# Sixteen loads of a state space layer kept in program order on GpSimd's DMA queue

## The chip, the cores and the metric

The kernel runs on one core of a Trainium2 chip. The core has five engines that work side by side, each through its own list of instructions in the order of that list: TensorE (PE in the profile; its weight loads are PEld), VectorE (DVE), ScalarE (ACT), GpSimd (POOL) and SyncE (SP, which here only issues DMAs). Sixteen DMA engines move data between the device memory and the on-chip memory; they serve DMAs issued from SP (queue q1 in the profile), from POOL (q0) and from ACT (q10). The metric is the device time of one execution in microseconds (us).

## The reference, cut to what matters

Four layers and then a fifth, more complex one act on 256 tokens of 1024 features. Each layer is a mixer and a gated feed-forward network (FFN) with a short convolution. The mixers of the first four layers are attention, spatial gating, a state space layer and attention. The state space layer is the one that the change touches:

```
def s5_layer(xn, w_in, lam_re, lam_im, log_dt, b_re, b_im, c_re, c_im, d_skip, w_glu):
    u = (xn @ w_in)                       # 64 groups of 16 inputs, 64 complex states each
    bu = einsum(bbar, u)                  # bbar from lam, dt, b
    x  = associative_scan(a, bu)          # along the 256 tokens
    y  = einsum(c, x).real + d_skip * u
    a, g = split(gelu(y) @ w_glu)
    return a * sigmoid(g)
```

## The kernel before, in words

**Stages.** `PHASES` lists eleven stages that run one after the other: sb0, ffn0, sgu, ffn1, s5, ffn2, sb3, ffn3, mix2, ffnx, ple. In all of them TensorE multiplies the activations, split in a high and a low part (`yh`, `yl`), with weights split in the same way (`wh`, `wl`), three products for each 128x128 block (`mm3`, lines 516 to 518).

**The weight stream.** All weights lie in device memory in the order of their use, in units of eight blocks, 512 KB each. SP loads one unit after the other into one of five staging tiles `st` (line 352). ScalarE rounds it to `wh` (line 374), VectorE subtracts to get `wl` (line 375), and the unit's 24 matmuls follow. A staging tile is free for the next load once its unit is split; units are split up to three ahead of the one in use.

**The preparation of the state space layer.** Much of that layer depends on its parameters alone. The generators `s5_pre`, `s5_pre2`, `s5_tables` and `s5_direct` are chained to one list of steps, and `pre_step` (line 419) traces a few of them at a time, at lower priority, between the work of the stages ahead of s5. They put three things in device memory: the output operators `dC`, the input operators `dB` (`s5_pre2`, line 1107) and the terms `dK`, the direct response of outputs to recent inputs.

**The input operators.** `s5_pre2` goes over eight pieces. For each it loads two tiles `A` of 512 KB over GpSimd's queue (lines 1116 and 1118; the next piece's loads are traced a piece ahead), combines them on VectorE in six operations (lines 1128 to 1136), and stores two tiles `O` of 256 KB to `dB`, again over GpSimd's queue (line 1138). The pools hold four `A` and three `O` tiles.

**The direct terms.** `s5_direct` (line 1196) comes last in the chain. It reads `dK` back in 16 loads of 256 KB, eight for each of the two tiles `dT`, over GpSimd's queue (line 1204). One load fills 16 partitions, each with 32 runs of 128 consecutive float32 values, that is runs of 512 bytes. The tiles are used by `y_mm(h, True)` at line 1302, the steps T0 and T1 of stage s5.

**What sets the order.** The program is traced once; the framework's scheduler then orders each engine's list by its own plan of when an instruction's inputs are there, and by priority. The order in which instructions were traced isn't kept, unless an edge says so. `issue_after(ins)` and `keep_in_program_order(ins)` add such edges. `keep_in_program_order` puts its instruction behind the last one that was traced on the same engine: an edge of issue order alone, without a wait for that instruction to end. In `pre_step`, steps of the preparation are put behind the last traced instruction of VectorE and of ScalarE, but not of GpSimd, so that GpSimd's DMAs of a later step can stand ahead of those of an earlier step.

Of the kernel before, what the change touches and what calls it, by code (L numbers as in the profile page):

```python
# [283 lines left out]
class Build:  # L284
# [911 lines left out]
    def s5_direct(s):  # L1196

        while s.cpT is None:
            yield None
        for h in range(2):  # L1200
            s.dT[h] = s.cpT.tile([128, 32, 128], F32, tag="dT%d" % h, name="dT")
            src = s.dK[h * 32:h * 32 + 32, 0:16].rearrange("g h z k -> h g (z k)")
            for j in range(8):
                s.nc.gpsimd.dma_start(s.dT[h][j::8], src[:, :, (8 - j) * 16:(8 - j) * 16 + 128])
                yield DTC

    def s5(s, nxt):
# [740 lines left out]
```

## Time and profile before

| | |
|---|---|
| median of 3 runs | 1618.14 us (1615.52 to 1618.92) |
| the profiled execution | 1621.75 us, of which 1619.9 us is the span from its first to its last instruction |
| TensorE busy | 1574.6 us, 97% of the span |
| VectorE busy | 1303.2 us, 80% |
| ScalarE busy | 948.5 us, 59% |
| GpSimd busy | 68.9 us, 4% |
| mean granted TensorE clock | 0.991 of full speed |
| moved by DMA | 312.55 MB, of which 27.12 MB on GpSimd's queue |

The shares are means over stages with different limits. Stage ffn1, in which the change acts, runs from about 395 to 585 us of the span; s5 follows. In a row of the trace the columns are start, duration, engine, line, operation, what it writes and reads, and in square brackets the time for which the engine stood idle just before it, with what ended that. Matmuls are pipelined: at full clock one ends every 0.11 us, though each is shown with about 0.28 us.

### The profile page before, as it was taken

To read this page: it belongs to the slowest core of one execution; us is meant where nothing else is said; L and a number is where in the kernel's file an instruction comes from. 1 tells how busy PE (TensorE), PEld (TensorE's weight loads), DVE (VectorE), ACT (ScalarE), POOL (GpSimd) and SP (SyncE) were. 2 spreads that over 40 slices of the span, in tenths; PEclk is the share of its full clock that TensorE was granted. 3 is DMA by queue.
4 is the path that set the end of the run, shared out by engine and by line. 5 is a ranking of instruction groups with operands and counts; after the bars stand their busy time and mean duration, and the time that the engine had idled before them with its cause. 6 is when DMAs were issued, how large, how long until landed. Compare 5 with 4: busy or idle time off the path is not lost.

```text
span 1619.9 us, 33923 instructions
## 1 busy us (share of the span) xinstructions
PE 1574.6 (97%) x13644; PEld 1512.5 (93%) x13644; DVE 1303.2 (80%) x2380; ACT 948.5 (59%) x1481; POOL 68.9 (4%) x118
## 2 busy tenths in 40 slices
PE   7999999989999997999999999999999999999998
PEld 6999999979999996999999999999997899999998
DVE  8999998888999877788788558988886667766666
ACT  6777665645556651666566676655665546554444
POOL 0320100021120000000000000000000000000000
PEclk9999999999999997999999999999999999999999
DMA  7655767697996666756665434666554434666662
GB/s 262 202 172 178 232 210 224 198 298 222 263 252 229 219 194 201 259 173 207 196 195 187 153 129 144 203 201 195 159 174 137 149 112 133 200 192 193 195 195 79
DMA packets 95359, 312.55 MB, mean 193 GB/s; under 512 B 15057, under 2 KB 20689, under 8 KB 95201
## 3 DMA queue, kind: packets, MB, share of 16 engines
q1 hardware_dynamic: 82560, 282.21, 55.1%
q0 software_dynamic: 8480, 27.12, 5.9%
q8 instruction: 107, 1.75, 0.4%
q10 hardware_dynamic: 4160, 1.05, 0.3%
q14 instruction: 52, 0.42, 0.1%
HBM read 297.49 MB, written 12.85 MB: 192 GB/s over the span
## 4 chain that ended last, share of the span: by engine, by line
PE 72%; DVE 10%; issue 9%; DMA 5%; ACT 3%; POOL 0%; DVEq 0%; POOLq 0%; ACTq 0%; SPq 0%
PE mm L516 16%; PE mm L518 15%; PE mm L517 15%; PE z L517 5%; PE z L516 5%; PE z L518 5%; DVE wl L375 3%; DMA A<-s5bT_dram 1%; DMA st<-ffn_dram 1%; PE mm L530 1%; PE mm L531 1%; PE mm L529 1%; ACT wh L374 1%; PE z L818 1%; PE z L805 1%
## 5 line engine op out<-in xcount | busy, mean ns | idle before, releaser
L375 DVE TENSOR_TENSOR wl<-st,wh 128x1024 fp32r<-128x1024 f32 x508 | 618.2, 1220 | 156.1 <-ACT wh L374 155.3
L374 ACT CAST wh<-st 128x1024 fp32r<-128x1024 f32 x508 | 528.7, 1046 | 328.0 <-PE mm L517 207.3
L516 PE MATMUL mm<-yh,wh 128*128 128x256 f32 x2512 | 703.7, 280 | 2.9 <-ACT yh L568 1.9
L517 PE MATMUL mm<-yl,wh 128*128 128x256 f32 x2512 | 698.6, 278 | 1.4 <-DVE yl L569 0.9
L518 PE MATMUL mm<-yh,wl 128*128 128x256 f32 x2512 | 698.4, 278 | 1.0 <-DVE wl L375 1.0
L516 PEld LDWEIGHTS mm<-yh,wh 128*128 128x128 f32 x2512 | 473.5, 189 | 10.7 <-issue 6.4
L517 PEld LDWEIGHTS mm<-yl,wh 128*128 128x128 f32 x2512 | 474.1, 189 | 3.3 <-DVE yl L569 1.7
L518 PEld LDWEIGHTS mm<-yh,wl 128*128 128x128 f32 x2512 | 474.1, 189 | 1.7 <-DVE wl L375 1.6
L516 PE MATMUL z<-hh,wh 128*128 128x256 f32 x880 | 243.6, 277 | 0.3 <-ACT hh L542 0.3
L517 PE MATMUL z<-hl,wh 128*128 128x256 f32 x880 | 243.0, 276 | 0.4 <-DVE hl L543 0.4
L518 PE MATMUL z<-hh,wl 128*128 128x256 f32 x880 | 242.1, 276 | 0.0
L516 PEld LDWEIGHTS z<-hh,wh 128*128 128x128 f32 x880 | 165.1, 188 | 1.4 <-ACT hh L542 0.5
L517 PEld LDWEIGHTS z<-hl,wh 128*128 128x128 f32 x880 | 165.2, 188 | 0.6 <-DVE hl L543 0.6
L518 PEld LDWEIGHTS z<-hh,wl 128*128 128x128 f32 x880 | 164.8, 188 | 0.0
L727 DVE SCALAR_TENSOR_TENSOR cv<-pr,conv,cv 128x255 f32<-128x255 f32 (+1 forms) x352 | 147.1, 480 | 0.4
L542 ACT CAST hh<-hm 128x256 fp32r<-128x256 f32 x110 | 44.4, 405 | 121.5 <-DVE hm L732 96.6
L725 ACT ACTIVATE cv<-pr,conv 128x256 f32<-128x256 f32 x176 | 95.7, 593 | 16.6 <-DVE pr L722 16.6
L516 PE MATMUL mm<-oh,wh 128*128 128x256 f32 x320 | 89.8, 282 | 0.0
L517 PE MATMUL mm<-ol,wh 128*128 128x256 f32 x320 | 88.2, 277 | 0.0
L518 PE MATMUL mm<-oh,wl 128*128 128x256 f32 x320 | 88.2, 277 | 0.0
L722 DVE TENSOR_TENSOR pr<-mm,rrow 128x512 f32<-128x512 f32 x88 | 60.3, 689 | 13.1 <-PE mm L518 12.9
L543 DVE TENSOR_TENSOR hl<-hm,hh 128x256 fp32r<-128x256 f32 x110 | 46.0, 422 | 22.7 <-ACT hh L542 22.5
(453 smaller groups left out, 1848.2 us busy)
## 6 DMA issues: line engine op xcount, KB each, us to landing
st<-ffn_dram SPq DMA_DIRECT2D x264, 512.0 KB, 4.3
st<-ffnx_dram SPq DMA_DIRECT2D x66, 512.0 KB, 3.6
st<-sbqk_dram SPq DMA_DIRECT2D x32, 512.0 KB, 4.0
st<-sbv_dram SPq DMA_DIRECT2D x16, 512.0 KB, 4.3
st<-sbo_dram SPq DMA_DIRECT2D x16, 512.0 KB, 3.5
st<-s5glu_dram SPq DMA_DIRECT2D x16, 512.0 KB, 6.1
st<-m_g_dram SPq DMA_DIRECT2D x16, 512.0 KB, 3.6
st<-ple_dram SPq DMA_DIRECT2D x10, 512.0 KB, 3.6
```

The source lines that it names most:

```text
L374: a = s.nc.scalar.copy(t[1][:, :n], t[0][:, :n])
L375: b = s.nc.vector.tensor_tensor(t[2][:, :n], t[0][:, :n], t[1][:, :n].bitcast(F32), OP.subtract)
L516: s.pinned(mm(P, w[0], xh, start=st, stop=False, skip_group_check=True))
L517: mm(P, w[0], xl, start=False, stop=False, skip_group_check=True)
L518: mm(P, w[1], xh, start=False, stop=sp, skip_group_check=True)
L529: s.pinned(mm(P[t][:, :width], a, w[0], start=c == 0, stop=False))
L530: mm(P[t][:, :width], a, w[1], start=False, stop=False)
L542: s.nc.scalar.copy(h, src)
L543: s.nc.vector.tensor_tensor(l, src, h.bitcast(F32), OP.subtract)
L722: nc.vector.tensor_tensor(pr, P, s.rrow.unsqueeze(1).to_broadcast([128, 2, T]), OP.mult)
L725: nc.scalar.activation(hc[:, m], pr[:, m], AF.Identity, bias=w(m, 3), scale=w(m, 2))
L727: nc.vector.scalar_tensor_tensor(hc[:, m, k:], pr[:, m, :T - k], w(m, 2 - k), hc[:, m, k:], OP.mult, OP.add)
```

## The change

Each of the sixteen `dT` loads gets an edge of issue order behind what was traced before it on GpSimd: the first behind the last store of `dB`, each other one behind the load before it.

```
--- before.py
+++ after.py
@@ -1201,7 +1201,8 @@
             s.dT[h] = s.cpT.tile([128, 32, 128], F32, tag="dT%d" % h, name="dT")
             src = s.dK[h * 32:h * 32 + 32, 0:16].rearrange("g h z k -> h g (z k)")
             for j in range(8):
-                s.nc.gpsimd.dma_start(s.dT[h][j::8], src[:, :, (8 - j) * 16:(8 - j) * 16 + 128])
+                s.tc.keep_in_program_order(
+                    s.nc.gpsimd.dma_start(s.dT[h][j::8], src[:, :, (8 - j) * 16:(8 - j) * 16 + 128]))
                 yield DTC
```

## Rows read from the trace of the kernel before

**Rows 1.** The page: busy time of the engines, and shares of the last chain
```profile
PE 1574.6 (97%) x13644; PEld 1512.5 (93%) x13644; DVE 1303.2 (80%) x2380; ACT 948.5 (59%) x1481; POOL 68.9 (4%) x118
PE 72%; DVE 10%; issue 9%; DMA 5%; ACT 3%; POOL 0%; DVEq 0%; POOLq 0%; ACTq 0%; SPq 0%
```
**Rows 2.** GpSimd's instructions in order of time, 390 to 600 us
```profile
390.84 0.56 POOL L1118 DMA_DIRECT2D A<-s5bT_dram  x1
396.92 1.26 POOL L1204 DMA_DIRECT2D dT<-dK  x2 [5.52 <-issue]
...
448.06 1.28 POOL L1204 DMA_DIRECT2D dT<-dK  x2
464.43 1.12 POOL L1138 DMA_DIRECT2D dB<-O  x2 [15.09 <-DVE O L1136]
465.55 1.28 POOL L1204 DMA_DIRECT2D dT<-dK  x2
467.39 3.71 POOL L1204 DMA_DIRECT2D dT<-dK  x6 [0.56 <-issue]
590.27 0.26 POOL L1225 MEMSET S<- 128x16 f32 x4 [119.17 <-PE z L518]
```
**Rows 3.** Tile dT: its uses and its loads (count: ns min/median/max, first and last start)
```profile
L1302 PE MATMUL z<-dT,U x128: 272/273/297, 617.7 to 635.2; 128*32 128x128 f32 x128
L1204 POOL DMA_DIRECT2D dT<-dK x16: 625/643/672, 396.9 to 470.5; - x16
```
**Rows 4.** VectorE's wait for loaded A tiles: sum, times and longest; the longest itself
```profile
DVE O L1128 <- DMA A<-s5bT_dram: 7.5, 3, 5.2
...
395.26 0.69 DVE L1128 TENSOR_TENSOR O<-A 128x512 f32<-128x512 f32 x1 [5.18 <-DMA A<-s5bT_dram]
```
**Rows 5.** Stretches: length, busy (count) by engine, PEclk, DMA share, GB/s
```profile
395.00:465.00 70.00, 65.97 (x544) 64.12 (x543) 68.19 (x127) 42.62 (x66) 11.13 (x20) 0.98 0.91 258
...
470.00:485.00 15.00, 15.00 (x135) 15.00 (x134) 12.24 (x26) 5.18 (x8) 1.10 (x2) 1.00 1.03 239
485.00:500.00 15.00, 13.59 (x114) 13.00 (x113) 14.52 (x25) 9.23 (x13) 0.00 (x0) 1.00 0.87 285
...
540.00:560.00 20.00, 20.00 (x179) 20.00 (x178) 17.40 (x28) 12.00 (x18) 0.00 (x0) 1.00 0.73 231
```
**Rows 6.** DMA queues from 470 to 485 us: packets, MB, share of 16 engines
```profile
q0 software_dynamic: 527, 1.72, 53.6%
q1 hardware_dynamic: 499, 1.85, 48.9%
```
**Rows 7.** ScalarE's rounding of weight units, order of time
```profile
471.73 1.05 ACT L374 CAST wh<-st 128x1024 fp32r<-128x1024 f32 x1
476.85 1.05 ACT L374 CAST wh<-st 128x1024 fp32r<-128x1024 f32 x1 [4.08 <-DMA st<-ffn_dram]
480.83 1.06 ACT L374 CAST wh<-st 128x1024 fp32r<-128x1024 f32 x1 [1.93 <-DMA st<-ffn_dram]
...
485.39 1.06 ACT L374 CAST wh<-st 128x1024 fp32r<-128x1024 f32 x1 [2.30 <-DMA st<-ffn_dram]
488.71 1.05 ACT L374 CAST wh<-st 128x1024 fp32r<-128x1024 f32 x1 [1.27 <-DMA st<-ffn_dram]
```
**Rows 8.** TensorE's waits behind that, order of time
```profile
487.76 0.39 PE L518 MATMUL mm<-yh,wl 128*128 128x256 f32 x1 [0.19 <-DVE wl L375]
491.62 0.39 PE L518 MATMUL mm<-yh,wl 128*128 128x256 f32 x1 [0.82 <-DVE wl L375]
```
**Rows 9.** Shorter stretches, columns as in rows 5
```profile
460.00:465.00 5.00, 5.00 (x47) 5.00 (x46) 5.00 (x9) 3.15 (x5) 0.57 (x2) 1.00 0.53 172
...
398.00:400.00 2.00, 0.92 (x6) 0.69 (x6) 2.00 (x6) 1.63 (x4) 0.19 (x1) 1.00 1.03 252
400.00:402.00 2.00, 1.06 (x4) 0.86 (x5) 2.00 (x5) 2.00 (x5) 0.00 (x0) 0.86 0.92 182
402.00:404.00 2.00, 2.00 (x12) 2.00 (x11) 2.00 (x5) 0.84 (x1) 0.00 (x0) 0.50 0.95 186
...
488.00:490.00 2.00, 2.00 (x19) 2.00 (x19) 2.00 (x6) 1.14 (x2) 0.00 (x0) 1.00 1.02 404
```

## The prediction

> **What bounds the kernel now.** I began with the page's busy times and its last chain: TensorE is busy for 97% of the span and carries 72% of the chain [rows 1]. So a change gains only what it takes from TensorE's few pauses, and costs what it adds to them. An average over the span doesn't say where the pauses are; so next I read GpSimd's list in order of time, to see where the moved loads stand. Of the sixteen `dT` loads the first two are issued at 396.92 us, right behind an `A` load of the input operators, and the last eight at 465.55 us and later, behind the last store of `dB` at 464.43 us [rows 2]. So eight of the sixteen are already where the change wants them, and the other eight go out between 397 and 450 us, ahead of or among the input operators' DMAs. All are there long before TensorE first reads them at 617.7 us [rows 3]. Then I read stretches around both halves. From 540 to 560 us, with no such load, TensorE does 179 matmuls in 20 us, 0.112 us each; a weight unit of 24 then takes 2.68 us, and the stream must bring 0.524 MB in that time, 196 GB/s [rows 5]. From 470 to 485 us, with the last eight `dT` loads under way, the sixteen DMA engines are full (share 1.03) and move only 239 GB/s [rows 5]: 1.85 MB for the stream, 123 GB/s, and 1.72 MB for GpSimd's queue, 115 GB/s [rows 6]. There the stream falls behind its consumer. ScalarE's roundings of the units are to be read as a clock of what arrives: from 471.73 to 485.39 us come three more units, 4.55 us apart, and each of the last four roundings shown waited for its own DMA [rows 7]. TensorE then waits for `wl` at 487.76 and 491.62 us [rows 8], and in the 15 us from 485 us it does 114 matmuls where 134 would fit: 2.2 us lost [rows 5].
>
> **The change part by part.** It removes no work. It moves eight loads, 2.10 MB, from the stretch 397 to 450 us to the end of the row that leaves from 465.55 us on, and adds no wait for an end. The issue itself is short: 0.643 us a load on GpSimd, 10.3 us for sixteen [rows 3]. Behind them on GpSimd stands nothing until a memset at 590.27 us [rows 2], so nobody queues behind the pinned loads; and moved past `dB` stores and `A` loads they free GpSimd for 5 us that it had to spare, as it idles 15.09 us ahead of the last stores alone [rows 2].
>
> What it **gives** is what the eight loads cost where they stood. The thing to ask is whether VectorE ever waited for an `A` tile that stood behind a `dT` load. It waited for `A` three times, 7.5 us in all; the longest wait, 5.18 us, ended at 395.26 us, before the first `dT` load was issued at 396.92 us [rows 2, 4]. It is the costly one, as the residual of the layer's end stands behind it on VectorE, but a load that isn't there yet can't have made it. I find no such wait behind a `dT` load, and so take 0 for this part. Its bounds: in the 70 us from 395 us TensorE does 544 matmuls where 627 would fit, so 9.2 us are lost there, to the end of one layer and the normalisation of the next [rows 5]. That is the most that a better order of VectorE's list could give back, as the scheduler makes its plan anew with the `A` tiles earlier in it; the same shuffle could cost something, and I put 2 us to that side, an estimate from the 2.2 us of the other disturbed stretch [rows 5].
>
> What it **costs** is a longer train of loads at the end: sixteen in a row where there were eight. Eight take 2.10 MB at 115 GB/s = 18.3 us, and in that time the stream runs at 123 of the 196 GB/s that it needs [rows 5, 6]. So each microsecond of the train puts the stream 1 - 123/196 = 0.37 us behind: 6.8 us for eight loads, 13.6 us for sixteen. The units in the staging tiles and those split ahead cover a part. How much, the train of before tells: 6.8 us of lag, 2.2 us of it lost on TensorE, so the cover was 4.6 us. With sixteen, 13.6 - 4.6 = 9.0 us are lost, 6.8 us more than before. The price from the roundings is close: at 4.55 us a unit [rows 7] the lag is 0.41 us per microsecond, 7.5 us for the eight that are added. From below: five staging tiles and three units split ahead are 8 x 2.68 = 21 us of weights, more than the whole lag. If all that were full and usable, nothing would be lost, and the 2.2 us of before would go too: -2.2 us. I take 6.8 us, because the train of before also began after a calm stretch (DMA share 0.53 from 460 to 465 us [rows 9]), when the stream had no more free tiles to fill, and still used its cover up.
>
> A starved TensorE may **lose its clock** too. Where it was busy for 0.92 and 1.06 of 2 us, at 398 to 402 us, the next 2 us were granted at 0.50, the lower of the two levels, 1.2 instead of 2.4 GHz, with 12 matmuls instead of 18: 0.7 us [rows 9]. In the train TensorE would work 2.68 of 4.3 us, 63%; from 485 to 500 us it did 85% of its work at 1.00 [rows 5]. This lies between the two; I take nothing for it, and up to 3 us (four such episodes) for the upper end.
>
> The lag lasts: behind the train TensorE is the bound again (20.00 of 20 us busy [rows 5]), so what it lost there ends the kernel later. The profiled execution took 1621.75 us, of it 1619.9 us span, 3.6 us above the median of 1618.14 us. On it the sum is 1621.75 + 6.8 = 1628.6 us; on the median, 1618.1 + 6.8 = 1624.9 us.
>
> A rule to weigh here is the cost of short runs. By rows, the stream alone moves 404 GB/s at 488 to 490 us [rows 9], and with the 512-byte runs of `dT` beside it both together get 239 GB/s [rows 5]. The Trainium skill, "DMA: Bandwidth & Descriptors", section Specifications, gives 512 bytes as the shortest transfer that still runs at line rate. By that rule the `dT` loads would be no slower than the stream's, and the lag would vanish; the rows above speak against it.
>
> **The rivals.** *The train is covered or harmless*: the time stays. One way is more cover: with eight loads fewer ahead of it the stream could enter the train with more units split. For it: 21 us of room. Against it: the calm stretch right before the old train. It would give between 1618.1 - 2.2 = 1615.9 and 1618.1 + 3.2 us; chance 0.12. Another way is that `dT` loads aren't the slow kind: at 404/2 = 202 GB/s for each queue [rows 9] the stream would have its 196 GB/s and lose nothing, 1615.9 us; against it stands the 239 GB/s at full DMA engines [rows 5]. This is where the rule on 512-byte runs would lead. Chance 0.05. The third is that the edges do little, because the plan for the first eight changes only on paper, and the train spreads: 1618 us, chance 0.05, as the edges are plain and half the loads must move.
>
> *Faster*: VectorE's backlog is what really makes TensorE late in both places, and the new plan removes it. VectorE is busy for 68.19 of 70 us from 395 us [rows 5], and the second wait of TensorE, at 491.62 us, was for a `wl` whose unit was rounded by 489.76 us, 488.71 + 1.05 [rows 7, 8]. If the operators' steps run earlier, the layer boundary gets back up to 9.2 us and the splits keep up in the train, which then costs between 0 and 6.8 us: 1609 to 1616 us, 1612 us in the middle. It decides from the point where an `A` tile that stood behind a `dT` load is on VectorE's path; I see none. Chance 0.10.
>
> **How the numbers follow.** Forecast 1624.9 us, chance 0.68; its own range is 1621.4 to 1630. Covered or harmless 0.12 + 0.05 + 0.05 = 0.22; faster 0.10. The range for 8 in 10 goes from 1616 us (the covered cases) to 1630 us (6.8 + 0.7 from the other pace + 3 for the clock, and 1.4 of the 2 us for a worse order); it leaves out most of the faster case and a little above. About 0.2%, 3.2 us, is what a measurement can tell from no change: faster by more 0.10, within it 0.22, slower by more 0.68.
>
> **What would show it.** All sixteen `dT` issues in one row on GpSimd behind the last `dB` store, some 10 us long, from about 465 us; DMA share at 1.0 with some 240 GB/s for about 37 us instead of 18 us; roundings of units some 4.3 to 4.5 us apart for nine units rather than four; TensorE some 9 us short of its matmuls between 485 and 515 us, against 2.2 us; the stretch 395 to 465 us unchanged at some 544 matmuls; the span's end later by what this stretch lost. It would be wrong if TensorE stays full through the train (more cover than I take), if the clock falls in it (more loss), or if the stretch 395 to 465 us holds clearly more matmuls (a better order of VectorE).

## The result, and the profile after

The changed kernel is slower, as forecast. Its median is 1623.95 us (8 runs, 1620.31 to 1628.46) beside 1615.8 us for the kernel before (8 runs, 1614.91 to 1618.92): the ratio is 1.0051, 95% interval 1.0039 to 1.0062, so +8.15 us, between +6.3 and +10.0. The profiled execution, the slowest of the eight, is counted for the kernel after and not for the one before; without it the difference is 7.5 us. Held against each other instruction by instruction, the two programs differ in GpSimd's list alone; TensorE, ScalarE, VectorE and SyncE have the same instructions in the same order.

| | before | after |
|---|---|---|
| median | 1615.8 us | 1623.95 us |
| profiled execution | 1621.75 us | 1628.46 us |
| its span | 1619.9 us | 1626.7 us |
| end of VectorE's longest wait for `A` to GpSimd's memset of `S` | 195.01 us | 203.54 us |

The last row is the stretch in which the `dT` loads run: it starts where the longest wait of [rows 4] ends, and ends with the memset at the end of [rows 2], which waits for the last product of the feed-forward layer. The first of its ends in the profile after is this row, VectorE in order of time:

```profile
395.81 0.69 DVE L1128 TENSOR_TENSOR O<-A 128x512 f32<-128x512 f32 x1 [5.22 <-DMA A<-s5bT_dram]
```

GpSimd's list in order of time, profile after (start, duration, line, operation; in brackets the idle time ahead of it and what ended it):

```profile
446.40 1.15 POOL L1138 DMA_DIRECT2D dB<-O  x2 [10.38 <-DVE O L1136]
462.52 0.54 POOL L1138 DMA_DIRECT2D dB<-O  x1 [14.98 <-DVE O L1135]
463.15 0.65 POOL L1205 DMA_DIRECT2D dT<-dK  x1
463.79 0.55 POOL L1138 DMA_DIRECT2D dB<-O  x1
464.33 3.75 POOL L1205 DMA_DIRECT2D dT<-dK  x6
468.56 0.64 POOL L1205 DMA_DIRECT2D dT<-dK  x1 [0.48 <-DMA dT<-dK]
470.44 0.62 POOL L1205 DMA_DIRECT2D dT<-dK  x1 [1.25 <-DMA dB<-O]
473.42 0.62 POOL L1205 DMA_DIRECT2D dT<-dK  x1 [2.35 <-DMA dT<-dK]
...
487.44 0.62 POOL L1205 DMA_DIRECT2D dT<-dK  x1 [1.73 <-DMA dT<-dK]
...
599.35 0.26 POOL L1226 MEMSET S<- 128x16 f32 x4 [111.28 <-PE z L518]
```

No `dT` load is left between 397 and 450 us [rows 2]. The first stands ahead of the last `dB` store, the other fifteen behind it: its edge is to the store that was traced last, which the scheduler issued first of the two, at 462.52 us. Seven go out at once; from the eighth on each is held back, seven of these nine by the landing of an earlier `dT` load, so that the issues last until 488 us. Nothing is queued behind them until the memset, which comes 9.1 us later than in [rows 2].

Stretches of the profile after, columns as in [rows 5], and below them the one of before that [rows 5] doesn't have:

```profile
395.00:465.00 70.00, 65.92 (x545) 64.10 (x545) 68.98 (x129) 42.83 (x67) 7.87 (x15) 0.98 0.76 238
...
470.00:485.00 15.00, 15.00 (x135) 15.00 (x133) 9.26 (x22) 5.07 (x8) 3.75 (x6) 1.00 1.03 228
485.00:500.00 15.00, 10.11 (x75) 8.82 (x74) 10.51 (x18) 5.18 (x8) 1.25 (x2) 1.00 1.04 237
500.00:520.00 20.00, 18.39 (x136) 18.10 (x137) 17.60 (x29) 14.30 (x20) 0.00 (x0) 0.83 0.79 238
...
540.00:560.00 20.00, 20.00 (x179) 20.00 (x178) 17.67 (x28) 13.22 (x21) 0.00 (x0) 1.00 0.66 212
```

```profile
500.00:520.00 20.00, 20.00 (x177) 19.83 (x176) 18.90 (x32) 15.72 (x22) 0.00 (x0) 1.00 0.62 202
```

From 395 to 465 us the count of matmuls is the same, 545 and 544; from 540 us on TensorE is full in both. Between 485 and 520 us, where 134 + 179 = 313 matmuls would fit, after does 75 + 136 = 211 and before 114 + 177 = 291: 102 and 22 short, at 0.112 us each 11.4 and 2.5 us, a difference of 9.0 us. That is where the time went. The DMA engines are full all the while (1.03, 1.04) and move 228 and 237 GB/s. By queue, 470 to 485 us (packets, MB, share of the 16 engines), profile after:

```profile
q0 software_dynamic: 510, 1.67, 54.5%
q1 hardware_dynamic: 470, 1.72, 48.4%
```

The stream gets 1.72 MB in 15 us, 115 of the 196 GB/s that it needs. ScalarE's roundings of weight units show the same, profile after, in order of time:

```profile
472.90 1.05 ACT L374 CAST wh<-st 128x1024 fp32r<-128x1024 f32 x1 [2.06 <-DMA st<-ffn_dram]
477.32 1.05 ACT L374 CAST wh<-st 128x1024 fp32r<-128x1024 f32 x1 [3.37 <-DMA st<-ffn_dram]
482.95 1.05 ACT L374 CAST wh<-st 128x1024 fp32r<-128x1024 f32 x1 [3.58 <-DMA st<-ffn_dram]
...
503.82 1.04 ACT L374 CAST wh<-st 128x1024 fp32r<-128x1024 f32 x1 [2.98 <-DMA st<-ffn_dram]
```

These are four of eight roundings, each after a wait for its own DMA: 7 intervals in 30.92 us, or 4.42 us a unit, where TensorE takes 2.68 us for one. TensorE's waits follow from 486.30 us on; two of the six in the profile after (the second is for `hh`, which ScalarE rounds only behind the late unit that it starts at 499.49 us):

```profile
486.30 0.39 PE L518 MATMUL mm<-yh,wl 128*128 128x256 f32 x1 [1.09 <-DVE wl L375]
...
500.90 0.58 PE L516 MATMUL z<-hh,wh 128*128 128x256 f32 x1 [2.89 <-ACT hh L542]
```

Behind the longest hole the clock falls, which before didn't happen here. Short stretches of the profile after:

```profile
500.00:502.50 2.50, 0.89 (x2) 0.60 (x3) 1.93 (x4) 0.84 (x2) 0.00 (x0) 0.60 1.03 231
502.50:505.00 2.50, 2.50 (x13) 2.50 (x13) 1.27 (x3) 1.18 (x2) 0.00 (x0) 0.50 1.01 270
505.00:507.50 2.50, 2.50 (x14) 2.50 (x14) 2.50 (x5) 2.01 (x4) 0.00 (x0) 0.54 1.04 408
```

From 502.5 to 507.5 us TensorE is never idle, but at a granted clock of 0.50 and 0.54, the lower level of 1.2 GHz, it does 27 matmuls where 5/0.112 = 44.6 would fit: 2.0 us of the 11.4, if the weights were there for more, which these rows don't show.

### The profile page after: what moved, and what is told of

Same layout as the page of the kernel before. It is cut to its first block, busy times and chain, and to the rows that moved or that the text cites. A ratio compares the mean times of both kernels' runs of the same rounds, so it can differ in the third digit from the quotient of the medians.

```text
span 1626.7 us, 33926 instructions
## 1 busy us (share of the span) xinstructions
PE 1577.5 (97%) x13644; PEld 1513.8 (93%) x13644; DVE 1303.7 (80%) x2380; ACT 948.8 (58%) x1481; POOL 68.8 (4%) x118
## 4 chain that ended last, share of the span: by engine, by line
PE 69%; DVE 10%; issue 10%; DMA 7%; ACT 3%; POOL 0%; SPq 0%; DVEq 0%; ACTq 0%; POOLq 0%
PE mm L516 15%; PE mm L518 15%; PE mm L517 15%; PE z L517 5%; PE z L516 5%; PE z L518 5%; DVE wl L375 4%; DMA st<-ffn_dram 2%; DMA A<-s5bT_dram 1%; PE mm L530 1%; ACT wh L374 1%; PE mm L531 1%; PE mm L529 1%; DMA st<-m_qk_dram 1%; DMA U<-dU 1%
```

## The experiments

**Theory:** the stream of weights starves in proportion to the train of `dT` loads behind the last store; beyond a cover that eight loads use up, each load costs some 0.85 us and more where the clock falls. **Rivals:** the order of the operators' transfers on GpSimd's queue has a price or gain of its own; the 512-byte runs of a load are what makes it slow; or the DMA engines are simply at their limit at some 240 GB/s.

Each edit is shown against the changed kernel. Beside medians (4 to 12 runs each) the runs are compared in the stretch of the table above, since profiled executions differ ahead of it by up to 4.5 us (its start lies between 391.29 and 395.81 us) although nothing is changed there. A stretch comes from a single profiled execution.

| kernel | stretch | against before | median against before, measured beside it | other engines' lists |
|---|---|---|---|---|
| after | 203.54 us | +8.5 | +8.15 | as before |
| twelve in the train | 198.64 us | +3.6 | +4.4 | as before |
| 32 loads | 213.15 us | +18.1 | +27.1 | changed |
| 16 KB runs | 204.89 us | +9.9 | +10.4 | as before |
| issued by ScalarE | 195.38 us | +0.4 | +8.5 | changed |
| 16 adjacent partitions | 214.83 us | +19.8 | +19.9 | as before |
| 128 partitions, 512-byte runs | 192.16 us | -2.9 | -5.0 | as before |
| 128 partitions, 64 loads of 64 KB | 192.17 us | -2.8 | -5.3 | as before |
| the same, without edges | 194.41 us | -0.6 | +0.5 | as before |
| loads spread in time | 192.32 us | -2.7 | +3.0 | changed |

Where only GpSimd's list differs, the median follows the stretch within 2.5 us. Where the scheduler made another list for TensorE, ScalarE or VectorE, the median is 6 to 9 us above it, lost behind the stretch (1032.4 to 1034.9 us from the memset to the end of the span, against 1023.4 to 1029.6 us with unchanged lists); such runs are read by the stretch alone. With 32 loads and with loads spread in time these lists part from those of before only at 585 us or later, behind the train or behind the stretch. With ScalarE as issuer they part at 491.9 us, and 14 matmuls fewer stand ahead of the memset, so that its stretch comes out some 1.6 us too short.

**Twelve loads behind the last store**, four left free.

```diff
-                dma(dB[pc, :, r], z.rearrange("p g q -> p (g q)"))
+                s.last_db = dma(dB[pc, :, r], z.rearrange("p g q -> p (g q)"))
...
-                s.tc.keep_in_program_order(
-                    s.nc.gpsimd.dma_start(s.dT[h][j::8], src[:, :, (8 - j) * 16:(8 - j) * 16 + 128]))
+                with s.tc.issue_after(s.last_db.ins) if h or j > 3 else nullcontext():
+                    s.nc.gpsimd.dma_start(s.dT[h][j::8], src[:, :, (8 - j) * 16:(8 - j) * 16 + 128])
```

> Only 12 of the 16 direct-term loads are put behind the last store of the input operators; the first four leave early, as before the change. Train theory (every load in the train puts the weight stream behind by 2.29 us x 0.37 = 0.85 us, some 1.0 us with the clock): 4 loads more in the train than before, 3 to 5 us over the kernel before, half of the change's 8.15 us. Rival threshold (the loss comes only once the train is as long as with 16): within 1 us of before. Rival place (the loss comes from the order among the input operators' transfers, which here is half kept): no reason for a half, 0 or 8 us.

Measured: 1619.79 us beside 1615.39 us, ratio 1.0031 (1.0018 to 1.0043). Stretches:

```profile
470.00:485.00 15.00, 14.17 (x125) 13.98 (x124) 10.56 (x20) 6.29 (x10) 1.88 (x3) 1.00 1.04 241
485.00:500.00 15.00, 11.95 (x90) 10.59 (x89) 12.31 (x22) 7.18 (x10) 0.00 (x0) 1.00 0.95 280
```

TensorE is 10 and 44 matmuls short of 135 and 134, and 2 more up to 520 us: 56, or 6.3 us, against 2.5 us with eight in the train and 11.4 us with sixteen. Half the added loads, about half the added time: the price is that of the number behind the store, not of the edge.

**Every load twice**, 32 in the train.

```diff
+        for h in (0, 1, 0, 1):
             src = s.dK[h * 32:h * 32 + 32, 0:16].rearrange("g h z k -> h g (z k)")
...
-                yield DTC
+                yield DTC / 2
```

> Every direct-term load is made twice, 32 in one train behind the last store. Train theory: 16 more loads x 2.29 us x 0.37 = 13.6 us more than the change's 8.15 us, and more pauses in which the clock may fall: 21 to 27 us over the kernel before. Rival once (the loss is a one-time price for emptying the staging tiles or for GpSimd's waits): 8 to 10 us over before, as with 16.

Measured: 1642.5 us beside 1615.39 us, 1.0171 (1.0154 to 1.0189). Stretches:

```profile
485.00:500.00 15.00, 9.61 (x58) 8.31 (x57) 8.80 (x15) 5.38 (x8) 4.51 (x7) 0.84 1.04 240
500.00:520.00 20.00, 18.16 (x140) 17.36 (x140) 13.09 (x22) 10.61 (x15) 5.14 (x9) 0.93 1.04 237
520.00:540.00 20.00, 16.87 (x123) 15.47 (x122) 11.90 (x19) 8.51 (x14) 0.49 (x1) 0.94 1.03 257
```

The full DMA engines and the starved TensorE last to 540 us. Stretch by stretch the sixteen loads more cost 18.1 - 8.5 = 9.6 us, 0.6 us each, somewhat under the 0.85 us of the prediction; the rest of the 27.1 us comes behind the stretch, where the lists are others, and no row ties it to the train.

**Long runs.** Sixteen runs of 16 KB a load instead of 512 bytes; `dT` gets other values.

```diff
-            src = s.dK[h * 32:h * 32 + 32, 0:16].rearrange("g h z k -> h g (z k)")
...
-                s.tc.keep_in_program_order(
-                    s.nc.gpsimd.dma_start(s.dT[h][j::8], src[:, :, (8 - j) * 16:(8 - j) * 16 + 128]))
+                g0 = h * 32 + (j % 4) * 8
+                src = s.dK[g0:g0 + 8].rearrange("g (a b) z k -> (g a) (b z k)", a=2).rearrange("p (g k) -> p g k", k=128)
+                s.tc.keep_in_program_order(s.nc.gpsimd.dma_start(s.dT[h][j::8], src))
```

> The 16 loads stay where the change puts them and carry the same 256 KB each, but read it as 16 runs of 16 KB in place of 512 runs of 512 bytes, from other addresses of the same tensor; so the values of the direct terms are others. Theory short runs (the train costs because 512-byte runs fill the DMA engines at 239 GB/s): the stream gets some 200 GB/s beside the loads and keeps up; the train takes some 21 us, and the time is 0 to 2 us under the kernel before. Rival shared queue (any second queue takes half of a fixed total of 240 GB/s): 8 us over before, as with short runs.

Measured: 1625.77 us beside 1615.39 us, 1.0068 (1.0055 to 1.008). One stretch, and its queues (packets, MB, share):

```profile
470.00:485.00 15.00, 11.51 (x98) 11.12 (x97) 4.93 (x11) 3.09 (x4) 2.89 (x6) 0.99 1.03 231
```

```profile
q0 software_dynamic: 292, 2.38, 69.8%
q1 hardware_dynamic: 291, 1.07, 32.4%
```

The total is what it was, 231 GB/s at full engines, so the short runs aren't what makes these loads slow. And the stream fares worse, 1.07 MB or 71 GB/s: the two queues take turns by packet (292 and 291), and the load's packets have grown to 8.2 KB beside the stream's 3.7 KB. The Trainium skill, "DMA: Bandwidth & Descriptors", section Queues, rings and completion order, says that a DMA engine goes round its queues a whole packet at a time; the equal counts agree.

**Sixteen adjacent partitions** instead of every eighth, same runs; the order of the rows in `dT` is another.

```diff
-                s.tc.keep_in_program_order(
-                    s.nc.gpsimd.dma_start(s.dT[h][j::8], src[:, :, (8 - j) * 16:(8 - j) * 16 + 128]))
+                s.tc.keep_in_program_order(s.nc.gpsimd.dma_start(s.dT[h][16 * j:16 * j + 16], src[:, :, (8 - j) * 16:(8 - j) * 16 + 128]))
```

> The changed kernel, each of the 16 loads with the same source, size and runs, but written to 16 adjacent partitions in place of every eighth one; so the rows of the direct terms stand in another order than the computation wants. Theory partitions (a load to 16 partitions is slow since few ways into the on-chip memory serve them; the Trainium skill, SBUF, section on the DMA port swizzle, puts every eighth partition on 8 ports and 16 adjacent ones on 4): packets of the train take about twice as long, the stream gets some 70 to 90 GB/s for some 50 us, 15 to 35 us over the kernel before. Rival shared queue (two queues share 240 GB/s whatever the destination): 8 us over before.

Measured: 1636.27 us beside 1616.41 us, 1.0127 (1.0113 to 1.014).

```profile
470.00:485.00 15.00, 12.62 (x108) 12.26 (x107) 6.29 (x13) 3.41 (x5) 3.15 (x5) 1.00 1.04 172
```

```profile
q0 software_dynamic: 366, 1.20, 52.7%
q1 hardware_dynamic: 364, 1.36, 50.8%
```

Only the destination has changed, and the full engines move 172 GB/s instead of 228; the stream has 91 GB/s left.

**All 128 partitions**, still runs of 512 bytes, four to a partition; `dT` gets other values.

```diff
-            src = s.dK[h * 32:h * 32 + 32, 0:16].rearrange("g h z k -> h g (z k)")
...
-                s.tc.keep_in_program_order(
-                    s.nc.gpsimd.dma_start(s.dT[h][j::8], src[:, :, (8 - j) * 16:(8 - j) * 16 + 128]))
+                e = s.dK[(j % 4) * 16:(j % 4) * 16 + 16]
+                src = bass.AP(tensor=e.tensor, offset=e.offset + 16 * j, ap=[[256, 128], [32768, 4], [1, 128]])
+                s.tc.keep_in_program_order(s.nc.gpsimd.dma_start(s.dT[h][:, 4 * j:4 * j + 4], src))
```

> The changed kernel, each of the 16 loads with the same size and 512-byte runs, but written to all 128 partitions, four runs each, from other addresses of the same tensor; so the values of the direct terms are others. Theory partitions: the train moves as fast as the weights do, the stream keeps some 200 GB/s beside it, no unit is late: 0 to 3 us under the kernel before. Rival shared queue: 8 us over before. Rival short runs: 8 us over before as well.

Measured: 1611.46 us beside 1616.41 us, 0.9975 (0.9964 to 0.9986): faster than before.

```profile
470.00:485.00 15.00, 15.00 (x135) 15.00 (x134) 14.74 (x31) 7.29 (x12) 4.53 (x7) 1.00 1.03 343
485.00:500.00 15.00, 15.00 (x134) 15.00 (x134) 13.98 (x24) 10.34 (x15) 0.00 (x0) 1.00 0.77 276
```

```profile
q0 software_dynamic: 740, 2.43, 51.7%
q1 hardware_dynamic: 740, 2.69, 50.7%
```

Same bytes, same runs, same edges: 343 GB/s, 179 of them for the stream, and TensorE does all its matmuls. Three destinations with 512-byte runs give 172, 228 to 239 and 343 GB/s at full DMA engines. So it is the partitions that a load writes to which set its pace, and the stream's beside it. This run also reads other addresses; the run ahead of it changes the destination alone, and the next one keeps the values of the kernel before. The Trainium skill, "SBUF — State Buffer", section Door 1: The DMA port swizzle, gives a reason that fits: a partition's number picks one of 16 ports, and a transfer has only the bandwidth of the ports that it reaches. By its formula sixteen adjacent partitions reach 4 ports, every eighth one 8, and all 128 reach 16. The three rates stand in that order; the page's 27.2 GB/s a port can't be read off, as no run had such a load without the stream beside it.

**All partitions, `dT` as in the kernel before**: 64 loads of 64 KB, one group each, the overlapping windows written into the source's strides.

```diff
-            src = s.dK[h * 32:h * 32 + 32, 0:16].rearrange("g h z k -> h g (z k)")
-            for j in range(8):
-                s.tc.keep_in_program_order(
-                    s.nc.gpsimd.dma_start(s.dT[h][j::8], src[:, :, (8 - j) * 16:(8 - j) * 16 + 128]))
-                yield DTC
+            for g in range(32):
+                e = s.dK[h * 32 + g]
+                src = bass.AP(tensor=e.tensor, offset=e.offset + 128, ap=[[256, 16], [-16, 8], [1, 128]])
+                s.tc.keep_in_program_order(s.nc.gpsimd.dma_start(s.dT[h][:, g], src))
+                if g % 4 == 3:
+                    yield DTC
```

> Each load of 256 KB to 16 partitions is replaced by four of 64 KB to all 128 partitions, one group each, 64 loads in all; values and runs of 512 bytes are those of the reference, the order behind the last store is that of the change. Theory partitions: 0 to 3 us under the kernel before, as the old train of eight goes too. Rival fixed cost (64 loads cost more than they save): GpSimd issues for 30 to 40 us, but the stream keeps its rate beside it: at most 2 us over before. Rival shared queue: 8 us over before.

Measured: 1611.11 us beside 1616.41 us, 0.9968 (0.9958 to 0.9978), 5.3 us faster than before; with the run ahead of it the fastest of all.

```profile
470.00:485.00 15.00, 15.00 (x135) 15.00 (x134) 14.96 (x27) 8.17 (x12) 9.53 (x18) 1.00 1.03 294
```

```profile
q1 hardware_dynamic: 854, 3.10, 70.7%
q0 software_dynamic: 628, 1.29, 31.8%
```

The stream has 207 GB/s, more than its 196, and nothing is lost up to 520 us. The stretch is 2.8 us shorter than before; of that the 2.5 us of the old train are accounted for. The other 2.5 of the 5.3 us lie outside the stretch and are not explained by a row.

**The same 64 loads, free**: the call is `s.nc.gpsimd.dma_start(s.dT[h][:, g], src)` without the edge.

> The 64 loads to all 128 partitions without the edges of the change, so that most of them leave among the input operators' transfers. Theory partitions: harmless there as well, within 2 us of the run with edges. Rival order (loads ahead of the input operators' transfers on GpSimd's queue make VectorE wait for its tiles): 2 to 8 us over the run with edges, with waits of VectorE for A tiles behind 397 us.

Measured: 1616.86 us beside 1616.41 us, 1.001 (0.9998 to 1.0021). The loads go out from 395.2 to 456.9 us. VectorE's waits on DMAs, 395 to 470 us (sum, times, longest):

```profile
DVE O L1135 <- DMA dB<-O: 3.3, 1, 3.3
```

So here the order on the queue does pay. With all loads ahead of the last stores, VectorE waits 3.3 us for an `O` tile whose `dB` store has not landed; it does not wait for an `A` tile, as the rival had it. TensorE does 34 and 38 matmuls in two stretches in which 47 each fit, 22 or 2.5 us short:

```profile
460.00:465.00 5.00, 3.76 (x34) 3.56 (x32) 2.15 (x4) 2.10 (x2) 0.77 (x2) 1.00 0.63 235
465.00:470.00 5.00, 4.33 (x38) 4.34 (x39) 5.00 (x9) 2.28 (x4) 0.31 (x1) 1.00 0.77 267
```

The stretch is 2.2 us longer than with the edges. The median is 5.8 us longer; the profiled execution is the fastest of its twelve, and what the others lose beyond the 2.2 us no row shows.

**Loads spread in time**: five memsets of a tile that holds nothing of use, behind each load on GpSimd.

```diff
+        pad = s.pre_big()
...
-                s.tc.keep_in_program_order(
-                    s.nc.gpsimd.dma_start(s.dT[h][j::8], src[:, :, (8 - j) * 16:(8 - j) * 16 + 128]))
+                s.tc.keep_in_program_order(s.nc.gpsimd.dma_start(s.dT[h][j::8], src[:, :, (8 - j) * 16:(8 - j) * 16 + 128]))
+                for _ in range(5):
+                    s.tc.keep_in_program_order(s.nc.gpsimd.memset(pad, 0.0))
```

> The changed kernel, with five memsets of a scratch tile on GpSimd behind each of the 16 loads, so that the same loads leave some 6 us apart in place of a train, over some 95 us from about 463 us on. Pacing theory: each load puts the stream 0.85 us behind, and in the 3.7 us up to the next one the stream, alone at well over 300 GB/s, makes that good; no unit is late, 0 to 3 us under the kernel before. Rival total (16 loads to every eighth partition cost 13.6 us of the stream's time wherever they stand, as the loads from ScalarE's queue in e4 suggest): 6 to 11 us over before. A side effect that the trace would show is VectorE slowed by the memsets.

Measured: 1618.67 us beside 1615.65 us, 1.0022 (1.001 to 1.0034). The loads, the changed kernel's own, go out some 6.3 us apart from 458.8 to 553.3 us. Two stretches, the second of them the 30 us from 45 us behind the memset of `S` on, and the same 30 us in the kernel before:

```profile
485.00:500.00 15.00, 15.00 (x135) 15.00 (x133) 15.00 (x26) 9.84 (x15) 14.48 (x15) 1.00 0.67 213
...
628.77:658.77 30.00, 23.59 (x233) 21.30 (x226) 23.31 (x37) 12.28 (x14) 0.95 (x1) 0.77 0.74 260
```

```profile
635.27:665.27 30.00, 26.26 (x285) 24.58 (x278) 21.33 (x32) 14.85 (x17) 0.95 (x1) 0.89 0.81 284
```

One slow load at a time leaves the stream enough, and TensorE loses nothing in the stretch (2.7 us shorter than before). The gain is lost behind it, in the state space layer, where TensorE does 233 matmuls against 285 at a lower granted clock (0.77 against 0.89), under another order of TensorE's, VectorE's and ScalarE's lists. The starving is shown to be one of loads in a row; as a version it doesn't pay.

**Issued by ScalarE**, free, with the loads' planned spacing and the number of side steps changed so that they fall into the feed-forward layer.

```diff
-DTC = 0.3
+DTC = 0.9
...
-FSIDE = ((0.2, 0.8, 15), (1.6, 0.2, 16))
+FSIDE = ((0.2, 0.8, 15), (1.6, 0.2, 22))
...
-                s.tc.keep_in_program_order(
-                    s.nc.gpsimd.dma_start(s.dT[h][j::8], src[:, :, (8 - j) * 16:(8 - j) * 16 + 128]))
+                s.nc.scalar.dma_start(s.dT[h][j::8], src[:, :, (8 - j) * 16:(8 - j) * 16 + 128])
```

> The 16 loads are issued by ScalarE, one or two for each feed-forward tile in place of a train, over the rest of the stage. Train theory: between two loads the stream catches up, no unit comes late; the pauses of the kernel before at its own train of eight go too: 1 to 3 us under before. Rival bandwidth (each load takes the stream's time wherever it stands): 13.6 us of lag in all, 6 to 11 us over before.

Measured: 1623.84 us beside 1615.39 us, 1.0059 (1.0046 to 1.0072). Queues from 540 to 580 us:

```profile
q1 hardware_dynamic: 1899, 6.92, 62.8%
q10 hardware_dynamic: 4751, 2.36, 34.0%
```

From 470 to 520 us nothing is lost, but the loads, thirteen of them from 525.9 us on and 4.5 us apart in the mean, fill the DMA engines again (0.94 and 1.00 from 540 to 580 us at 230 and 237 GB/s), and three lists are others. From 520 to 580 us TensorE does 489 matmuls where 537 would fit, 5.4 us short. Of ScalarE's roundings there a single one waited for its DMA, for 0.9 us, while ScalarE waited 26.7 us for VectorE, with roundings behind such waits in its new list; so the weights were there and the rounding was late. The run says that the place of the train was the cause in 485 to 520 us, and no more.

## Why the prediction was right

**The sign and the main term stand.** The train of sixteen starves the stream, at the rate that the train of eight showed: 4.42 us a unit against a forecast of 4.3 to 4.5; full DMA engines from 465 to 507 us, some 42 us against 37; nothing else changed, as VectorE's list is the same. The lag without the clock cost TensorE 11.4 - 2.0 = 9.4 us, against a forecast of 9.0. The dose of loads (2.5, 6.3, 11.4 us short with 8, 12 and 16) bears out that the cover was used up at eight, so "covered or harmless" fell.

**The clock was mis-sized.** I took nothing for it and kept 3 us for the range; it fell once, for 2.0 us. That, on the 6.8 us, makes 8.8 us; measured are 9.0 in lost matmuls, 8.5 in the stretch and 8.15 in the medians.

**The gain of 0 stands on TensorE, not quite on VectorE.** From the end of the longest wait for `A` to the paired `dB` stores at 446 us it was 51.66 us before and is 50.59 us after, within 0.02 us the same in each kernel with none of these loads in that place or with four of them (with the 64 free ones it is 64.84 us). The start before is in [rows 4], the end is this row of GpSimd, profile before:

```profile
446.92 1.16 POOL L1138 DMA_DIRECT2D dB<-O  x2 [10.16 <-DVE O L1136]
```

But TensorE gets little of it. Stretches that begin 20 and 52 us behind that wait, before and then after:

```profile
415.26:447.26 32.00, 30.89 (x266) 30.27 (x265) 30.77 (x60) 20.09 (x32) 6.42 (x12) 1.00 0.96 266
447.26:463.26 16.00, 16.00 (x141) 15.90 (x141) 15.68 (x26) 9.33 (x15) 2.06 (x4) 1.00 0.77 241
```

```profile
415.81:447.81 32.00, 30.89 (x266) 30.28 (x265) 31.79 (x62) 21.44 (x33) 4.66 (x9) 1.00 0.80 242
447.81:463.81 16.00, 16.00 (x143) 16.00 (x143) 16.00 (x27) 9.44 (x15) 1.20 (x3) 1.00 0.67 215
```

266 and 266 matmuls, then 141 and 143: 0.2 us. The rival "faster" fell with that: VectorE waited for `A` 8.0 us in all after against 7.5 us before [rows 4], and its list wasn't planned anew.

**The issue was not one row of 10 us.** It lasts 25 us, since each load from the eighth on waits for an earlier DMA to land. This cost nothing, as the engines were full either way; it stretched what the trace shows.

**The reason that I gave for the loads' pace was wrong.** The prediction held 239 GB/s at full engines against the page's rule that 512 bytes already run at line rate, and took the short runs for the cause. Long runs didn't help and wide destinations with short runs went at 343 GB/s. The Trainium skill, "DMA: Bandwidth & Descriptors", section Specifications, was right on this, as far as these runs show; what was slow was the set of partitions. The forecast survived because it used the measured rate of the same loads. The rival built on the rule, that the stream keeps its 196 GB/s and 1615.9 us come out, came near what happened once the destination was wide: 179 to 207 GB/s for the stream, and 1611 us, 5.0 to 5.3 us under the kernel before where the rival had 2.2.

**That the profiled execution came out at 1628.46 us, where 1628.6 was forecast, is partly luck:** +0.55 us ahead of the stretch, +8.53 in it and -2.30 behind it. The last is within what profiled executions with the same lists differ there (1023.4 to 1029.6 us). The median of 1623.95 us beside a forecast of 1624.9 is luck too: the forecast stood on a median of three runs that was 2.3 us above that of eight, and this made up for a rise that came out at 8.15 us instead of 6.8.

**Open** stays what makes the time behind the stretch differ, with unchanged lists by up to 6 us and with other lists by more; why all-partition loads win 5 us where the stretch shows 2.8, and why a load beyond the sixteenth cost 0.6 us and not 0.85.

## What to carry to other kernels

A transfer that is moved off a crowded place is paid for where it lands: take the rate that is left to the weight stream there, from the queues' rows while such loads run, and price the whole train by it, with the cover that the train before had used up. Before moving a slow load, look at which partitions it writes; here the same bytes over all 128 turned a change that costs 8 us into one that gains 5, and only then was the order itself worth something. Full DMA engines at a low rate don't mean that the limit is reached.

## What the runs showed of the hardware

- Beside the weight stream, at DMA shares of 1.03 to 1.04, loads of 512-byte runs gave a total of 172 GB/s into 16 adjacent partitions, 228 to 239 into every eighth, and 343 into all 128 (294 when they came as loads of 64 KB). The slow destination takes the stream down with it (91, 115 to 123, 179 GB/s).
- The two queues shared by packets, not by bytes, when both had work all the time: 292 and 291 packets, 2.38 and 1.07 MB; 740 and 740, 2.43 and 2.69 MB. Larger packets took the larger share.
- The same kind of load went out in packets of 3.3 KB when GpSimd issued it (1.67 MB in 510), and of 0.5 KB when ScalarE did (2.36 MB in 4751).
- GpSimd ran ahead by seven `dT` loads and then waited at each next one for an earlier DMA to land, 10.5 us in seven waits on `dT` loads.
